# Joint heads of a hybrid S5 / RG-LRU trunk: the square behind T3's sum, a copy of Z behind the gates' sigmoids, results stored from `sq`, rows fetched back sooner, and head 9's gates on single banks

## The chip, the cores and the metric

The kernel runs on one core of one Trainium2 chip. The metric is device time in microseconds. The core has five engines that each work through their own instructions in order: TensorE (PE in the profile; its weight loads are PEld), VectorE (DVE), ScalarE (ACT), GpSimd (POOL) and SyncE (SP). They wait for one another through semaphores. SyncE and GpSimd here mostly start DMA transfers.

## The reference, cut to what matters

```python
proj = rms_norm(x, g_pre) @ w_in           # x: (1, 1024, 1024), w_in: 1024 x 5632
s5_x, s5_g, lru_x, lru_g, gate_s, gate_l = split(proj)
...
c = causal_depthwise_conv(lru_x, conv_w, conv_b)              # width 4
r = sigmoid(c_head @ w_a[head] + b_a)                         # 10 heads of 128 channels
i = sigmoid(c_head @ w_x[head] + b_x)
a = exp(-8 * r * softplus(-lam))
h = scan(h * a + sqrt(1 - a * a) * (i * c))                   # along 1024 tokens
z_l = (h * silu(lru_g)) @ w_bl
merged = sigmoid(gate_s) * z_s + sigmoid(gate_l) * z_l
x = x + rms_norm(merged @ w_out, g_post)
x = x + (p @ w_ple) * sigmoid(x @ w_ple_gate)
```

Everything is float32. The change touches only the LRU branch: the projections to `lru_x` and `lru_g`, the convolution, the gates `r` and `i`, the scan, and the way the heads' results reach the product with `w_bl`.

## The kernel before

Channels lie on the 128 partitions and the 1024 tokens in the free dimension, in two halves of 512. A 512-column float32 result fills one bank of the matmul accumulator (PSUM, 8 banks). To keep float32 accuracy every operand is split into a high part (a rounded copy made by ScalarE) and a low part (the difference, made by VectorE or by an accumulating DMA), and every product is three matmuls: high by high, high by low, low by high (`three`, L343 to 347).

**Weights.** A "quad" is four 128x128 blocks. `Weights` loads raw blocks with SyncE (L184, tile `wraw`), copies the high part on ScalarE (L246, tile `wq`), and makes the low part on VectorE (L260), or, for some, on ScalarE and GpSimd (L251, L252). `W.ahead(held)` makes quads in advance, as far as a ring of six allows; a larger `held` makes one quad fewer in advance. The instructions that it issues stand in each engine's order at that place of the program.

**Heads.** Ten heads, m = 0 to 9, run one behind the other. Heads 0, 1, 3, 4, 6 and 7 are *joint* (`joint_head`): the `lru_x` block and the `lru_g` block of a head are taken together, with the two halves of tokens, as one 2x2 block product in seven products instead of eight. Each product is a quad by 512 tokens, 12 matmuls, in this order: B11 into `c11`, T2 into `z`, B21 into `c11`, T1 into `c12`, T3 into `z`, B22 into `c12`, T4 into `z`. `c11` and `c12` are the two halves of the wide tile `hx`, `z` is the single-bank tile `hz`. Between the products sums are formed: z + u (L1358), a copy of z into `u` (ScalarE, L1359), c12 + u (L1372), and `gb` + z (VectorE, L1378), which reads T3's result before T4 adds to the same bank. `u` and `gb` are the halves of the tile `ug`. Heads 2, 5, 8 and 9 are *plain* (`plain_head`): two products of 48 matmuls each, `rx` and `rg`.

**What a head does behind its products** runs beside the products of the next head. The convolution reads `hx` (ScalarE L1268, then three steps on VectorE L1271) and gives `c`; `split` cuts it into high and low parts, `chl`. The gates are four groups of three matmuls, `pg`: the first half of tokens between T2 and B21 of the next head (in a plain head between the two halves of `rx`), the second half between T1 and T3. Their sigmoids (L1306) give `r` and `i`. Then `decay`: tanh into `ta` (L1313), exp into `r` (L1314), a square into `sq` (L1315). Then `root` (L1318, L1319), `scaled` (L1322), `scan` into `sq` (L1325) and `out`: product with the gate into `ta` (L1333), and a store of `ta` to DRAM on GpSimd's queue (L1334). `r`, `i`, `ta` and `sq` exist once, so each head waits for the one before to be done with them. `upto(n)` runs the first n of these steps, and `late` spreads them over the ticks of a plain head.

**Rows back from DRAM.** The results of heads 0 to 7 go to `yr_d`. At the start of head 9 all eight rows are fetched on GpSimd's queue (L1414) into four pages of two rows; `yr_build` splits and subtracts them (L340, L341, L1419, L1422) as operands of the product with `w_bl`, whose first four products are `bX`.

**Accumulator banks.** Pool `px` has two single banks, pool `pw2` two wide tiles (two banks each) and two single ones. The gates use `px`, except the second half of head 9, which takes a wide tile.

Of the kernel before, what the change touches and what calls it, by code (L numbers as in the profile page):

```python
# [9 lines left out]
F32 = mybir.dt.float32  # L10
F32R = mybir.dt.float32r
I32 = mybir.dt.int32
AF = mybir.ActivationFunctionType
ALU = mybir.AluOpType
# [3 lines left out]
P = 128  # L18
NT = 1024
HT = 512  # L20
ND = 8
NS = 4
NL = 10
# [14 lines left out]
JOINT = (0, 1, 3, 4, 6, 7)  # L38
# [118 lines left out]
class Weights:  # L157
# [104 lines left out]
    def next(self):  # L262
        self.make(self.pos)
        self.lows(self.pos)
        t = self.done[self.pos]
        n = QUADS[self.pos][3]
        self.pos += 1
        return [(t[:, 0, b, :], t[:, 1, b, :]) for b in range(n)]
# [10 lines left out]
def tile_hybrid_trunk(  # L279
# [10 lines left out]
    nc = tc.nc  # L290
    V, S, G, T = nc.vector, nc.scalar, nc.gpsimd, nc.tensor
# [3 lines left out]
    px = ctx.enter_context(tc.tile_pool(name="px", bufs=2, space=PSUM))  # L295
# [6 lines left out]
    def page(i, name, dt=F32R):  # L302
        return page_pool[i].tile([P, 2 * NT], dt, tag=f"pg{i}", name=name)
# [10 lines left out]
    yr_d = dram.tile([ND, P, NT], F32, name="yr_d")  # L314
# [22 lines left out]
    HALF = [slice(0, HT), slice(HT, NT)]  # L337
# [11 lines left out]
    def wide(name):  # L349
        return pw2.tile([P, NT], F32, tag="pw2", name=name)  # L350
# [6 lines left out]
    def tick():  # L357
        for g in list(bg):
            if next(g, bg) is bg:
                bg.remove(g)  # L360
# [132 lines left out]
    def xt(k, s=slice(0, NT)):  # L493
        return x_half[k // 4][:, k % 4, s]

    def two_rows(i, name, dt=F32):
        return page(i, name, dt).rearrange("p (k n) -> p k n", k=2)
# [258 lines left out]
    def square(k):  # L756
        sq = sqs[k % 2][:, k // 2 % 2] if k else ssq
        if k in (1, 3):
            (V if k == 1 else G).tensor_tensor(sq, xt(k), xt(k), ALU.mult)
        else:  # L760
            S.activation(sq, xt(k), AF.Square)
        if k:
            adds.append(sq)
# [333 lines left out]
    lop = {"T2": [3, 19], "T1": [16, 17], "T3": [2, 15], "T4": [7, 8]}  # L1097
# [45 lines left out]
    def lprod(ps, op, start, held=1):  # L1143
        W.ahead(held)
        for k, wb in enumerate(W.next()):
            three(ps, wb, (op[0][:, k, :], op[1][:, k, :]), start and k == 0, k == 3, not start)
# [20 lines left out]
    def lt(tag, name):  # L1167
        return la.tile([P, NT], F32, tag=tag, name=name)
# [35 lines left out]
    def gbank(i, name):  # L1204
        return gps.tile([P, HT], F32, tag=f"gb{i % 6}", name=name)

    for p_, m in enumerate(PAIRS):
        z = gbank(2 * p_, f"lZ{p_}") if p_ < 3 else px.tile([P, HT], F32, tag="px", name="lZ3")
# [3 lines left out]
        u = lu[:, p_]  # L1212
# [20 lines left out]
    def single(name):  # L1233
        return pw2.tile([P, HT], F32, tag="one", name=name)

    yl, yl_raw = {}, {}
    yr = []
    chl_page = page(6, "chl").rearrange("p (s n) -> p s n", s=2)
    gpage = two_rows(9, "gpage")
    ug = lt("ug", "ug")  # L1240
    u, gb = (ug[:, HALF[i]] for i in range(2))
# [14 lines left out]
    class Head:  # L1256
# [38 lines left out]
        def gates(self, h):  # L1295
            m = self.m
            if h == 0:
                self.held = W.next()
                self.r, self.i = lt("r", f"r{m}"), lt("i", f"i{m}")
            both = wide(f"pg{m}{h}") if h and m == NL - 1 else None  # L1300
            pss = [px.tile([P, HT], F32, tag="px", name=f"pg{m}{h}") if both is None else both[:, HALF[n]]
                   for n in range(2)]
            for ps, b in zip(pss, self.held):
                three(ps, b, (self.chl[:, 0, HALF[h]], self.chl[:, 1, HALF[h]]), True, True)
            for ps, t, bias in zip(pss, (self.r, self.i), (b_a, b_x)):
                S.activation(t[:, HALF[h]], ps, AF.Sigmoid, bias=bias[:, m:m + 1])  # L1306
            if h:
                V.tensor_tensor(self.i, self.i, self.c, ALU.mult)

        def decay(self):  # L1310
            m = self.m
            self.ta, self.sq = lt("ta", f"ta{m}"), lt("sq", f"sq{m}")
            S.activation(self.ta, self.r, AF.Tanh, scale=sp8[:, m:m + 1])  # L1313
            S.activation(self.r, self.r, AF.Exp, scale=nsp8[:, m:m + 1])  # L1314
            S.activation(self.sq, self.r, AF.Square)  # L1315

        def root(self):
# [9 lines left out]
        def out(self):  # L1327
            m = self.m
            if self.last:
                yl_raw[m] = lb[0].tile([P, NT], F32, tag=f"yr{m}", name=f"yr{m}")  # L1330
                V.tensor_tensor(yl_raw[m], self.sq, self.g, ALU.mult)
            else:
                V.tensor_tensor(self.ta, self.sq, self.g, ALU.mult)  # L1333
                G.dma_start(yr_d[m], self.ta)  # L1334

        def upto(self, n):
            while self.at < n:
                (self.decay, self.root, self.scaled, self.scan, self.out)[self.at]()
                self.at += 1

        def late(self):
            for n in (1, 2, 4, 5):
                self.upto(n)
                yield

    heads = {}

    def joint_head(m):
        head, prev, old = heads[m], heads.get(m - 1), heads.get(m - 2)
        xw, z = wide(f"hx{m}"), single(f"hz{m}")  # L1350
        c11, c12 = (xw[:, HALF[i]] for i in range(2))
        lprod(c11, hq["B11"], True)
        S.activation(u, c11, AF.Copy)
        if prev:
            prev.split()
        tick()
        lprod(z, lop["T2"], True)
        V.tensor_tensor(z, z, u, ALU.add)  # L1358
        S.activation(u, z, AF.Copy)  # L1359
        if old:  # L1360
            old.upto(4)
        if prev:
            prev.gate()
            prev.gates(0)
        tick()
        lprod(c11, hq["B21"], False, 1 + bool(prev))
        if old:
            old.upto(5)
        tick()
        lprod(c12, lop["T1"], True, 1 + bool(prev))  # L1370
        S.activation(gb, c12, AF.Copy)
        V.tensor_tensor(c12, c12, u, ALU.add)  # L1372
        if prev:
            prev.gates(1)
            prev.upto(1)
        tick()
        lprod(z, lop["T3"], False)
        V.tensor_tensor(gb, gb, z, ALU.add)  # L1378
        tick()
        lprod(c12, hq["B22"], False)  # L1380
        head.conv(xw, (lambda: prev.upto(2)) if prev else lambda: None)
        tick()
        lprod(z, lop["T4"], False)
        if prev:
            prev.upto(3)
        tick()
        head.parts = [(HALF[1], gb), (HALF[0], z)]

    def plain_head(m):
        head, prev, old = heads[m], heads.get(m - 1), heads.get(m - 2)  # L1390

        def between(q):
            if q:
                prev.gates(1)
                bg.append(prev.late())
                return False
            old.upto(5)
            if not prev.last:
                prev.gate()
            prev.gates(0)  # L1400
            return True

        if prev.unsplit:
            bg.insert(0, prev.first())
        head.conv(rows(hplain, f"rx{m}", between=between))
        bg.append(head.early())
        head.parts = [(slice(0, NT), rows(hplain, f"rg{m}"))]
        if head.last:
            head.gate()

    def yr_row(k):
        if k % 2 == 0:
            yr.append(two_rows(6 + k // 2, f"yr{k // 2}"))
        G.dma_start(yr[k // 2][:, k % 2], yr_d[k])  # L1414

    def yr_build():
        for k in range(4):
            bsplit("B11", k, bq(11, k))
            V.tensor_tensor(bq(11, k), bq(12, k), bq(11, k), ALU.subtract)  # L1419
            yield  # L1420
        for k in range(4):
            V.tensor_tensor(bq(12, k), bq(22, k), bq(12, k), ALU.subtract)  # L1422
            yield

    for m in range(NL):
        heads[m] = Head(m)
        if m == JOINT[-1] + 1:
            tctx.close()
            lb.append(lctx.enter_context(tc.tile_pool(name="lb", bufs=1)))
        if m == NL - 1:  # L1430
            heads[m - 2].upto(5)
            for k in range(ND):
                yr_row(k)
            bop("B11", 2, 3)
            bg.append(yr_build())
        (joint_head if m in JOINT else plain_head)(m)
# [9 lines left out]

    def between(q):
        if q == 0:
            heads[NL - 2].upto(5)
            for h in range(2):  # L1450
                heads[NL - 1].gates(h)
            bg.append(heads[NL - 1].late())
# [174 lines left out]
    for p_ in range(4):  # L1627
        m, u = 2 * p_, bu[:, p_, :]
# [8 lines left out]
        z, w_, v = (bank(f"b{n}{p_}") for n in "ZWV")  # L1637
# [202 lines left out]
    for p_ in range(4):  # L1840
        u, c21, c22 = mixt(2 * p_, 1), mixt(2 * p_ + 1, 0), mixt(2 * p_ + 1, 1)
# [173 lines left out]
```

## Time and profile before

| | us |
|---|---|
| median of 3 runs | 934.56 |
| lowest and highest run | 933.51, 934.73 |
| the profiled execution | 935.66 |
| its span, first to last instruction | 933.9 |
| TensorE busy in the span | 903.8 (97%) |
| VectorE busy | 694.0 (74%) |
| ScalarE busy | 524.9 (56%) |
| GpSimd busy | 132.4 (14%) |
| mean granted TensorE clock | 0.987 |

The heads run from about 301 to 575 us of the span. A matmul of 512 columns starts every 0.227 us when nothing is in its way. In rows of the timeline the first two numbers are the start and the time taken in us; then come the engine, the line, the operation, the tiles (out<-in), their shapes and how many instructions the row merges. In square brackets is how long the engine had been idle before, and what ended that. In the view of waits the three numbers are the total, the times and the longest, in us.

### The profile page before, as it was taken

How to read it: one execution, taken by the hardware profiler on the slowest of the kernel's cores; microseconds unless marked ns; L12 is line 12 of the kernel's file. 1: busy time of each engine (PE TensorE's matmuls, PEld its weight loads, DVE VectorE, ACT ScalarE, POOL GpSimd, SP SyncE). 2: the span in 40 equal slices, each digit the busy share in tenths (PEclk: the TensorE clock that was granted, in tenths of full speed). 3: DMA queues.
4: the chain of work that ended last, by engine and by line, in shares of the span. 5: the costliest groups of instructions: out<-in, count | busy, mean ns of one | idle time of the engine just before them, and what ended most of it. 6: DMA issues, size and time to landing. Idle time of an engine off the chain costs nothing.

```text
span 933.9 us, 11840 instructions
## 1 busy us (share of the span) xinstructions
PE 903.8 (97%) x4108; PEld 743.9 (80%) x4108; DVE 694.0 (74%) x1135; ACT 524.9 (56%) x825; POOL 132.4 (14%) x154
## 2 busy tenths in 40 slices
PE   8999999999999999889988989999999999999998
PEld 6888888888788878678767877888888888887886
DVE  6988988899745566677777777877873698786863
ACT  6644345546744486775777677544534256558531
POOL 1311000011000000000000100012322115422100
PEclk9999999999999999999989999999999999999999
DMA  9776776666654321332222255731469976499951
GB/s 358 302 254 168 230 223 182 195 177 209 167 170 147 100 70 46 97 96 74 68 67 85 97 202 158 248 135 35 158 216 268 240 200 214 120 235 242 273 200 58
DMA packets 80620, 158.34 MB, mean 170 GB/s; under 512 B 19376, under 2 KB 33840, under 8 KB 80560
## 3 DMA queue, kind: packets, MB, share of 16 engines
q1 hardware_dynamic: 54208, 112.10, 35.9%
q0 software_dynamic: 10656, 24.12, 11.7%
q10 hardware_dynamic: 15696, 21.37, 7.8%
q8 instruction: 32, 0.52, 0.2%
q14 instruction: 28, 0.23, 0.1%
HBM read 105.78 MB, written 35.91 MB: 152 GB/s over the span
## 4 chain that ended last, share of the span: by engine, by line
PE 66%; issue 15%; ACT 7%; DVE 7%; DMA 3%; POOL 1%; SPq 0%; POOLq 0%; ACTq 0%; DVEq 0%
PE ps_L L347 9%; PE ps_L L345 4%; PE ps_pg L347 3%; PE ps_F L347 3%; PE ps_u L347 3%; PE bZ L347 3%; PE lZ L347 2%; PE bW L347 2%; PE bX L347 2%; PE ps_pg L345 2%; PE hz L347 2%; PE ps_rx L347 2%; PE ps_ea L347 2%; PE ps_eb L347 2%; PE ps_F L345 2%
## 5 line engine op out<-in xcount | busy, mean ns | idle before, releaser
L246 ACT ACTIVATE wq<-wraw 128x512 fp32r<-128x512 f32 (+1 forms) x192 | 115.1, 612 | 42.2 <-DMA wraw<-w_blocks 12.0
L260 DVE TENSOR_TENSOR wq<-wraw,wq 128x512 fp32r<-128x512 f32 (+1 forms) x136 | 94.9, 706 | 36.3 <-ACT wq L246 36.2
L347 PE MATMUL ps_L<-hB,wq 128*128 128x512 f32 x384 | 119.3, 392 | 0.0
L252 POOL DMA_DIRECT2D wq<-wraw x56 | 49.3, 885 | 274.0 <-ACT wq L251 195.7
L347 PEld LDWEIGHTS ps_L<-hB,wq 128*128 128x128 f32 x384 | 72.9, 190 | 15.3
L345 PE MATMUL ps_L<-hB,wq 128*128 128x512 f32 x192 | 76.4, 398 | 0.0
L347 PE MATMUL ps_pg<-x1hl,wq 128*128 128x512 f32 x240 | 74.6, 392 | 0.9 <-DVE x1hl L1691 0.5
L347 PEld LDWEIGHTS ps_pg<-x1hl,wq 128*128 128x128 f32 x240 | 44.7, 188 | 11.7 <-DVE x1hl L1691 2.0
L347 PE MATMUL hz<-lT,wq 128*128 128x512 f32 x144 | 49.5, 428 | 0.0
L345 PE MATMUL ps_pg<-x1hl,wq 128*128 128x512 f32 x120 | 46.9, 391 | 0.0
L345 PE MATMUL hz<-lT,wq 128*128 128x512 f32 x72 | 31.4, 435 | 14.4 <-DVE ug L1378 14.4
L347 PE MATMUL hx<-hB,wq 128*128 128x512 f32 x144 | 44.5, 390 | 0.0
L345 PEld LDWEIGHTS ps_L<-hB,wq 128*128 128x128 f32 x192 | 36.4, 190 | 7.4
L347 PE MATMUL ps_u<-hB,wq 128*128 128x512 f32 x128 | 39.8, 392 | 0.4 <-DVE hB L787 0.4
L347 PE MATMUL ps_rg<-hB,wq 128*128 128x512 f32 x128 | 39.9, 393 | 0.0
L347 PE MATMUL ps_rx<-hB,wq 128*128 128x512 f32 x128 | 39.4, 389 | 0.0
L347 PE MATMUL ps_F<-ys,wq 128*128 128x512 f32 x128 | 39.4, 389 | 0.0
L260 DVE TENSOR_TENSOR wq<-wS,wq 128x512 fp32r<-128x512 f32 x50 | 35.6, 716 | 5.0 <-ACT wq L246 5.0
L246 ACT ACTIVATE wq<-wS 128x512 fp32r<-128x512 f32 x50 | 31.2, 626 | 8.8 <-POOL wS L217 7.6
L347 PEld LDWEIGHTS hz<-lT,wq 128*128 128x128 f32 x144 | 30.4, 211 | 6.7
L251 ACT ACTIVATE wq<-wraw 128x512 fp32r<-128x512 f32 x56 | 34.7, 620 | 0.0
L347 PEld LDWEIGHTS hx<-hB,wq 128*128 128x128 f32 x144 | 27.3, 190 | 5.7
(428 smaller groups left out, 2349.8 us busy)
## 6 DMA issues: line engine op xcount, KB each, us to landing
wraw<-w_blocks SPq DMA_DIRECT2D x99, 512.0 KB
wq<-wraw POOLq DMA_DIRECT2D x56, 256.0 KB, 4.1
xt<-x_t SPq DMA_DIRECT2D x8, 512.0 KB
ple_d<-ple_sb SPq DMA_DIRECT2D x8, 512.0 KB
h_d<-xt SPq DMA_DIRECT2D x8, 512.0 KB
wn<-sbt ACTq DMA_DIRECT2D x8, 512.0 KB
wn<-pt_d ACTq DMA_DIRECT2D x16, 256.0 KB
fT<-h_d ACTq DMA_DIRECT2D x4, 1024.0 KB
```

Of the source, the lines that this page charges most:

```text
L246: nc.scalar.activation(hi, src, AF.Copy)
L251: nc.scalar.activation(lo, src, AF.Copy, scale=-1.0)
L252: nc.gpsimd.dma_start(lo.bitcast(F32), src, accum_op=ALU.add)
L260: self.nc.vector.tensor_tensor(lo, src, hi.bitcast(F32), ALU.subtract)
L345: T.matmul(ps, wh, xh, start=start, stop=False, skip_group_check=more)
L347: T.matmul(ps, a, b, start=False, stop=stop and a is (wh if xl_last else wl), skip_group_check=more)
```

## The change

There are five edits.

- `square` becomes a step of its own. In a joint head T3 now leaves one more quad unmade (`held` is 2), the sum L1378 (now L1379) follows, and the square comes behind both. The steps' numbers rise by one.
- The copy of z into `u` (L1359, now L1365) moves behind the gate's and the first gates' sigmoids.
- `out` multiplies in place, in `sq`, and stores `sq` on SyncE's queue, not `ta` on GpSimd's.
- The rows are fetched page by page: rows 2 to 5 at the start of head 8, rows 0 and 1 behind head 7's second gates, rows 6 and 7 at the start of head 9. `yr_build` takes them in the order 2, 3, 0, 1.
- The second gates of head 9 use two single banks of `pw2`.

On VectorE, in head 1 as the current and head 0 as the one whose gates are formed, from c12's sum on (`hx`, `hz`: this head's products; `i`, `c`, `ta`, `sq`: head 0; `wq`: weights):

```order
-L1372 TENSOR_TENSOR hx_2991<-hx_2991,ug 128x512
-L1308 TENSOR_TENSOR i_3035<-i_3035,c_2964 128x1024
-L260 TENSOR_TENSOR wq_3100<-wraw_2917,wq_3100 128x512
-L1378 TENSOR_TENSOR ug<-ug,hz_2992 128x512
-L260 TENSOR_TENSOR wq_3102<-wraw_2974,wq_3102 128x256
-L1318 SCALAR_TENSOR_TENSOR ta_3095<-sq_3096,ta_3095 128x1024
+L1373 TENSOR_TENSOR hx_2991<-hx_2991,ug 128x512
+L1307 TENSOR_TENSOR i_3034<-i_3034,c_2964 128x1024
+L1379 TENSOR_TENSOR ug<-ug,hz_2992 128x512
+L260 TENSOR_TENSOR wq_3099<-wraw_2917,wq_3099 128x512
+L260 TENSOR_TENSOR wq_3115<-wraw_2974,wq_3115 128x256
+L1319 SCALAR_TENSOR_TENSOR ta_3095<-sq_3096,ta_3095 128x1024
```

The sum into `ug` stood behind the low part of a weight and now stands ahead of it. On ScalarE at the same place, before:

```order
L1315 ACTIVATE sq_3096<-r_3034 128x1024
L246 ACTIVATE wq_3100<-wraw_2917 128x512
L246 ACTIVATE wq_3102<-wraw_2974 128x256
L246 ACTIVATE wq_3118<-wraw_2917 128x512
L1268 ACTIVATE c_3135<-hx_2991,cp_t 128x1024
```

and now:

```order
L246 ACTIVATE wq_3099<-wraw_2917 128x512
L1316 ACTIVATE sq_3096<-r_3033 128x1024
L246 ACTIVATE wq_3115<-wraw_2974 128x256
L246 ACTIVATE wq_3117<-wraw_2917 128x512
L1268 ACTIVATE c_3135<-hx_2991,cp_t 128x1024
```

The square has changed places with the copy of the next product's weight; the five instructions are otherwise the same. On ScalarE in head 3, around the first gates (`gpage`: the gate of head 2, `pg`: its gates' products):

```order
 L1292 ACTIVATE gpage<-ps_rg_3260 128x1024
-L1306 ACTIVATE r_3375<-pg_3377,cp_t 128x512
-L1306 ACTIVATE i_3376<-pg_3378,cp_t 128x512
+L1305 ACTIVATE r_3374<-pg_3376,cp_t 128x512
+L1305 ACTIVATE i_3375<-pg_3377,cp_t 128x512
+L1365 ACTIVATE ug<-hz_3339 128x512
```

The copy out of `hz`, which stood ahead of the gate (L1359), now stands behind `r` and `i`. On SyncE, the stores of heads 0 and 1 among the loads of weights:

```order
 L184 DMA wraw_3216<-w_blocks 128x1024
+L1335 DMA yr_d<-sq_3096 128x1024
 L184 DMA wraw_3218<-w_blocks 128x1024
 L184 DMA wraw_3307<-w_blocks 128x256
-L184 DMA wraw_3446<-w_blocks 128x1024
+L1335 DMA yr_d<-sq_3280 128x1024
+L184 DMA wraw_3442<-w_blocks 128x1024
```

A store now stands between loads that followed each other directly. The diff, cut to its core:

```diff
-            both = wide(f"pg{m}{h}") if h and m == NL - 1 else None
-            pss = [px.tile([P, HT], F32, tag="px", name=f"pg{m}{h}") if both is None else both[:, HALF[n]]
-                   for n in range(2)]
+            both = h and m == NL - 1
+            pss = [single(f"pg{m}{h}") if both else px.tile([P, HT], F32, tag="px", name=f"pg{m}{h}") for _ in range(2)]
...
             S.activation(self.r, self.r, AF.Exp, scale=nsp8[:, m:m + 1])
+
+        def square(self):
             S.activation(self.sq, self.r, AF.Square)
...
-                V.tensor_tensor(self.ta, self.sq, self.g, ALU.mult)
-                G.dma_start(yr_d[m], self.ta)
+                V.tensor_tensor(self.sq, self.sq, self.g, ALU.mult)
+                nc.sync.dma_start(yr_d[m], self.sq)
...
         V.tensor_tensor(z, z, u, ALU.add)
-        S.activation(u, z, AF.Copy)
         if old:
-            old.upto(4)
+            old.upto(5)
         if prev:
             prev.gate()
             prev.gates(0)
+        S.activation(u, z, AF.Copy)
         tick()
...
-        lprod(z, lop["T3"], False)
+        lprod(z, lop["T3"], False, 1 + bool(prev))
         V.tensor_tensor(gb, gb, z, ALU.add)
+        if prev:
+            prev.upto(2)
         tick()
...
                 prev.gates(1)
                 bg.append(prev.late())
+                if prev.m == JOINT[-1]:
+                    yr_rows(0)
                 return False
...
-    def yr_row(k):
-        if k % 2 == 0:
-            yr.append(two_rows(6 + k // 2, f"yr{k // 2}"))
-        G.dma_start(yr[k // 2][:, k % 2], yr_d[k])
+    def yr_rows(n):
+        yr[n] = two_rows(6 + n, f"yr{n}")
+        for i in range(2):
+            G.dma_start(yr[n][:, i], yr_d[2 * n + i])
...
-        for k in range(4):
+        for k in (2, 3, 0, 1):
             bsplit("B11", k, bq(11, k))
...
+            yr_rows(1)
+            yr_rows(2)
         if m == NL - 1:
-            heads[m - 2].upto(5)
-            for k in range(ND):
-                yr_row(k)
+            heads[m - 2].upto(6)
+            yr_rows(3)
```

More of the change, by code (lines that the diff above doesn't have):

```diff
@@ L1236, in tile_hybrid_trunk @@
     yl, yl_raw = {}, {}
-    yr = []
+    yr = {}
     chl_page = page(6, "chl").rearrange("p (s n) -> p s n", s=2)
@@ L1332, in out @@
             else:
-                V.tensor_tensor(self.ta, self.sq, self.g, ALU.mult)
-                G.dma_start(yr_d[m], self.ta)
+                V.tensor_tensor(self.sq, self.sq, self.g, ALU.mult)
+                nc.sync.dma_start(yr_d[m], self.sq)
         def upto(self, n):
             while self.at < n:
-                (self.decay, self.root, self.scaled, self.scan, self.out)[self.at]()
+                (self.decay, self.square, self.root, self.scaled, self.scan, self.out)[self.at]()
                 self.at += 1
         def late(self):
-            for n in (1, 2, 4, 5):
+            for n in (2, 3, 5, 6):
                 self.upto(n)
@@ L1367, in joint_head @@
         if old:
-            old.upto(5)
+            old.upto(6)
         tick()
@@ L1376, in joint_head @@
         tick()
-        lprod(z, lop["T3"], False)
+        lprod(z, lop["T3"], False, 1 + bool(prev))
         V.tensor_tensor(gb, gb, z, ALU.add)
+        if prev:
+            prev.upto(2)
         tick()
         lprod(c12, hq["B22"], False)
-        head.conv(xw, (lambda: prev.upto(2)) if prev else lambda: None)
+        head.conv(xw, (lambda: prev.upto(3)) if prev else lambda: None)
         tick()
@@ L1384, in joint_head @@
         if prev:
-            prev.upto(3)
+            prev.upto(4)
         tick()
@@ L1395, in between @@
                 bg.append(prev.late())
+                if prev.m == JOINT[-1]:
+                    yr_rows(0)
                 return False
-            old.upto(5)
+            old.upto(6)
             if not prev.last:
@@ L1448, in between @@
         if q == 0:
-            heads[NL - 2].upto(5)
+            heads[NL - 2].upto(6)
             for h in range(2):
```

## The prediction

> **What bounds the kernel now.** I read the waits of TensorE first, cut to the stretch from 300 to 600 us in which the ten LRU heads run. The columns are total us, times, longest.
>
> ```profile
> PE hz L345 <- DVE ug L1378: 14.4, 5, 3.2
> PE pg L345 <- ACT r L1306: 4.5, 3, 2.8
> PE pg L345 <- DVE g L1293: 2.2, 1, 2.2
> ```
>
> Five times, once in each joint head behind the first, T4 stands before VectorE's sum L1378, which must read T3's result out of `hz` before T4 may add to it. Then I read busy time by stretches (busy us of PE, PEld, DVE, ACT, POOL, then the granted TensorE clock and DMA).
>
> ```profile
> 300.00:600.00 300.00, 278.99 (x1174) 227.09 (x1173) 214.18 (x247) 209.66 (x286) 18.14 (x27) 0.96 0.34 106
> 338.96:342.37 3.41, 1.54 (x8) 0.97 (x7) 2.49 (x4) 3.39 (x6) 0.00 (x0) 1.00 0.00 0
> 342.37:345.79 3.42, 3.42 (x10) 2.68 (x9) 3.35 (x4) 2.80 (x4) 0.00 (x0) 0.50 0.12 38
> 495.97:499.39 3.42, 1.72 (x8) 1.10 (x6) 0.10 (x1) 3.38 (x5) 0.00 (x0) 1.00 0.48 153
> 499.39:502.80 3.41, 2.07 (x9) 1.78 (x10) 3.41 (x5) 3.38 (x5) 0.00 (x0) 1.00 0.15 41
> ```
>
> TensorE is the bound: 279.0 of 300 us busy, 21.0 idle, and the clock's 0.04 below 1 costs another 12 us (give or take 1.5 for the rounding). So 33 us of this stretch are lost. The four short rows show how an idle spell lowers the clock: 1.54 us busy in a 3.41 us stretch is followed by a stretch at half clock, which loses 1.7 us; 1.72 us busy is not. I take it that 1.8 us of idleness within one such stretch is the point. **A page speaks against these rows.** The Trainium skill, "TensorE: Matmul & The Clock Gate", section "HAM oscillation — how this bites in real kernels", sets the rule that only gaps above about 3.4 us matter. The 1.87 us wait quoted next brought half clock, so the trace disagrees.
>
> **The change, T4's wait.** I worked through head 1's stage. TensorE: T3, B22, T4, and the next head's first product.
>
> ```profile
> 333.84 0.39 PE L345 MATMUL hz<-lT,wq 128*128 128x512 f32 x1
> ...
> 336.56 0.39 PE L345 MATMUL hx<-hB,wq 128*128 128x512 f32 x1
> ...
> 341.32 0.47 PE L345 MATMUL hz<-lT,wq 128*128 128x512 f32 x1 [1.87 <-DVE ug L1378]
> ...
> 345.67 0.45 PE L345 MATMUL ps_rx<-hB,wq 128*128 128x512 f32 x1
> ```
>
> ScalarE and VectorE in the same stage:
>
> ```profile
> 333.36 0.69 ACT L1306 ACTIVATE r<-pg,cp_t 128x512 f32<-128x512 f32 x1
> ...
> 337.08 1.15 ACT L1314 ACTIVATE r<-r,nsp 128x1024 f32<-128x1024 f32 x1
> 338.27 1.06 ACT L1315 ACTIVATE sq<-r 128x1024 f32<-128x1024 f32 x1
> 339.24 1.44 ACT L246 ACTIVATE wq<-wraw 128x512 fp32r<-128x512 f32 x3
> 340.58 1.19 ACT L1268 ACTIVATE c<-hx,cp_t 128x1024 f32<-128x1024 f32 x1
> ```
>
> ```profile
> 334.77 1.23 DVE L1308 TENSOR_TENSOR i<-i,c 128x1024 f32<-128x1024 f32 x1 [0.75 <-ACT i L1306]
> 339.88 0.69 DVE L260 TENSOR_TENSOR wq<-wraw,wq 128x512 fp32r<-128x512 f32 x1 [3.89 <-ACT wq L246]
> 340.49 0.68 DVE L1378 TENSOR_TENSOR ug<-ug,hz 128x512 f32<-128x512 f32 x1
> 341.09 0.42 DVE L260 TENSOR_TENSOR wq<-wraw,wq 128x256 fp32r<-128x256 f32 x1
> 341.42 1.22 DVE L1318 SCALAR_TENSOR_TENSOR ta<-sq,ta 128x1024 f32<-128x1024 f32 x1
> 342.56 3.91 DVE L1271 SCALAR_TENSOR_TENSOR c<-hx,cp_t,c 128x1023 f32<-128x1023 f32 x3
> ...
> 348.72 0.69 DVE L217 TENSOR_TENSOR wS<-wraw 128x512 f32<-128x512 f32 x1
> 349.44 0.69 DVE L217 TENSOR_TENSOR wS<-wS,wraw 128x512 f32<-128x512 f32 x1
> 350.06 1.28 DVE L341 TENSOR_TENSOR chl<-c,chl 128x512 fp32r<-128x512 f32 x2
> ```
>
> A product of 12 matmuls takes 336.56 - 333.84 = 2.72 us. Today the sum is queued on VectorE behind a weight's low part, which idles 3.89 us for ScalarE: exp ends at 338.2, the square follows, and only then the weight's copy. With one weight fewer made ahead of T3, the sum comes first: L1308 ends at 336.0, T3 at 336.6, so the sum runs from about 336.8 to 337.5. B22 ends at 336.56 + 2.72 = 339.28, so T4 no longer waits. It also loses its slow clock: today T4 takes 345.67 - 341.32 = 4.35 us. The weight that is made later is still in time: copied behind exp, its low part is done by 339.5, and T4 covers it until 342.0.
>
> **What is late next: the gates.** T4 would run 339.28 to 342.00, the next head's first 24 matmuls to 347.44, and then the gates' first half. Its second matmul, at 347.67, is the first to read the low part of `chl`, the convolution's split output. ScalarE does the same work ahead of `c` in another order, so `c` still starts at 340.5 and ends at 341.7. VectorE is rid of the sum there: low part at 338.8, the 0.42 one behind its copy at about 340.1, `ta` 340.4 to 341.6, convolution at 341.7 instead of 342.56, 0.87 earlier. What stands between convolution and `chl` is unchanged, so `chl`'s first half ends at 350.06 + 0.69 - 0.87 = 349.9 (0.69 as the other 128x512 rows), and with the 0.15 us from 341.17 (the sum's end) to 341.32 TensorE goes on at 350.0. **A new wait of 2.35 us** stands where none was. Said generally: from `r` (333.36) to that second matmul TensorE has 14.31 us of work, and the chain needs 16.7.
>
> Head 4 has the same list of instructions (2.4, a trifle for `r`, which must wait for the scan of the head before). Head 7 lacks the two additions L217, 1.4 us, which leaves 1.0. Heads 3 and 6:
>
> ```profile
> 385.90 0.70 ACT L1306 ACTIVATE r<-pg,cp_t 128x512 f32<-128x512 f32 x1
> ...
> 402.16 1.29 DVE L341 TENSOR_TENSOR chl<-c,chl 128x512 fp32r<-128x512 f32 x2 [0.31 <-ACT chl L340]
> ```
>
> 402.16 + 0.69 - 385.90 = 16.95, less 0.87, plus 0.15, is 16.2; against 14.31 about 1.8 is left, 1.7 because part of the 0.31 goes too. Five new waits: 2.35 + 1.7 + 2.4 + 1.7 + 1.0 = **9.15 us**. The ends for this unknown: nothing, if the chain shortens by more than I see, and T4's present 14.4 us if it shortens by nothing.
>
> Half clock: the waits of 2.35 and 2.4 hold 1.8 us of idleness within one 3.41 us stretch in about 6 of 10 positions (TensorE's idle time is some 0.15 less than the wait: (1.6 + 0.4) / 3.41). I take one such stretch, 1.7 us; the ends are none and five. The other three waits are too short. By the rule of the Trainium skill named above none of the five would lower the clock, which would give 1.7 us less.
>
> **Copy of Z behind the sigmoids.** In heads 3 and 6 ScalarE is held by that copy:
>
> ```profile
> 379.89 0.60 ACT L1359 ACTIVATE ug<-hz 128x512 f32<-128x512 f32 x1 [5.62 <-DVE hz L1358]
> ```
>
> The sigmoids that free the gates' banks stood behind it; they now run within these 5.62 us. So the two shorter waits on `r` go: 4.5 - 2.8 = 1.7 us. T3, which overwrites what the copy reads, comes three products later (2.72 + 2.72 + 1.36 = 6.8 us behind the gates), which hides the move; without that cover T3 would wait for the copy's 0.60 us.
>
> **Rows fetched sooner.** Head 8's gates waited 2.8 us because ScalarE stood at a split of fetched rows:
>
> ```profile
> 540.70 0.63 ACT L340 ACTIVATE bB<-yr 128x512 fp32r<-128x512 f32 x1 [9.36 <-DMA yr<-yr_d]
> ```
>
> The rows that this split reads first are now asked for when head 7's T4 frees their pages, so a plain head ahead: 24 + 24 + 48 matmuls and two gates are 21.8 + 2.7 = 24.5 us. The 2.8 us go. **Head 9 on single banks:** its second gates no longer wait for the wide tile that L1293 releases; the pool's single banks were last used by head 7. The 2.2 us go, and what follows (L7's second half, 24 matmuls or 5.4 us) covers the reading of the singles before bX0 writes there.
>
> **Sum.** All 33 us go; 9.15 of new waits and 1.7 of half clock come: 33 - 10.85 = 22.15. Against the profiled execution: 935.66 - 22.15 = 913.5. The median of the runs lies 1.1 below that execution, so **912.4 us**.
>
> **Rivals.**
> *The new wait doesn't come* (chance 0.10): if VectorE or ScalarE have slack that I did not see, 33 us go: 934.56 - 33 = 901.6. Against it: every row of head 1's chain follows its predecessor without a gap.
> *The wait only moves* (0.14): every new wait is 1 us longer and lowers the clock: 9.15 + 5 + 5 x 1.7 = 22.65, gain 10.3, 924.2. For it: ScalarE and VectorE get fuller when the stretch shrinks; the 1.7 us waits are only 0.3 from the point. That the early fetch does nothing, because a page comes free later than I think, would cost 2.8 + 1.7 alone, within the range.
> *No half clock follows* (0.04): if waits this short leave the clock alone, 9.15 us come and no more: 33 - 9.15 = 23.85, 910.7. The stretch with 1.54 us busy, which brought half clock, speaks against it. That is what the rule in the Trainium skill, "TensorE: Matmul & The Clock Gate", would make of these waits.
> *Slower: the stores on SyncE's queue* (0.04). Each store of a head's rows now stands between weight loads, and the next square, in the same `sq`, waits for it on ScalarE. Head 1's loads on either side, and the product it stores:
>
> ```profile
> 372.80 6.25 SPq L184 DMA_DIRECT2D wraw<-w_blocks  x2
> ...
> 376.82 1.22 DVE L1333 TENSOR_TENSOR ta<-sq,gpage 128x1024 f32<-128x1024 f32 x1
> ```
>
> ```profile
> yr_d<-ta POOLq DMA_DIRECT2D x7, 512.0 KB, 2.9
> ```
>
> The load ahead went at 372.80, before the product ended at 378.04; the one behind at 372.80 + 6.25 - 0.33 = 378.72. The store fits between. The square comes at least T1, gates and T3 later (6.8 us), the store needs 2.9. It would decide from a store held 3.9 us, and the kernel would be slower once all eight were held 3.9 + 22.15 / 8 = 6.7 us; at 10 us each the time is 912.4 + 8 x 6.1 = 961.
>
> **Chances.** 0.68 for the forecast, whose own range is 908 to 917. The range for 8 in 10 takes in most of the moved wait and part of the missing one: 905 to 922. What this kernel's measurement can tell from no change is 0.2%, 1.9 us: faster 0.94, same 0.02, slower 0.04.
>
> **What would show it.** The profile after should have no wait of `hz` on the sum; a wait of `pg` on `chl` (L341), five times, 1 to 2.5 us, about 9 in all, first at the gates of head 1; one or two stretches at clock 0.50 where there were seven (12 / 1.7); no wait of `pg` on `r` or `g`; on ScalarE no square waiting for a store. The forecast is wrong if T4 still waits, if `chl` waits 3 us or more each time, or if loads on SyncE land late and `wq` appears among TensorE's waits.

## The result, and the profile after

| | before | after |
|---|---|---|
| median, us | 934.03 (4 runs, 933.44 to 934.73) | 913.03 (4 runs, 912.93 to 913.75) |
| ratio after to before | | 0.9776, 95% interval 0.976 to 0.9793 |
| the profiled execution, us | 935.66 | 913.0 |
| span, us | 933.9 | 911.2 |

The kernel is 21.0 us faster, where 22.15 was forecast; the time, 913.03, stands 0.6 us from the predicted 912.4. Between the two profiled executions, from which the forecast was worked out, the gain is 22.7 us. The agreement hides errors in what each edit was held to be worth, which the experiments bring out.

TensorE's waits after the change, from 300 to 600 us (total, times, longest):

```profile
PE pg L347 <- DVE chl L341: 7.8, 5, 2.1
```

This one line stands where three stood. T4 waits no more for the sum, and the gates no more for `r` or `g`; the gates wait five times for the low part of `chl`. The engines' busy times by stretches (PE, PEld, DVE, ACT, POOL, clock, DMA):

```profile
300.00:600.00 300.00, 292.23 (x1277) 240.19 (x1276) 230.91 (x266) 217.38 (x297) 18.35 (x23) 0.99 0.39 120
347.35:350.76 3.41, 1.34 (x7) 0.79 (x5) 3.38 (x6) 2.40 (x3) 0.00 (x0) 1.00 0.53 154
350.76:354.18 3.42, 3.42 (x10) 2.64 (x9) 3.38 (x3) 0.92 (x2) 0.00 (x0) 0.50 0.00 0
419.02:422.43 3.41, 3.04 (x14) 2.19 (x12) 3.41 (x5) 2.75 (x5) 0.00 (x0) 1.00 0.27 56
422.43:425.84 3.41, 1.70 (x7) 1.42 (x8) 3.38 (x5) 1.07 (x2) 0.00 (x0) 1.00 0.26 102
```

TensorE idles 7.8 of the 300 us, down from 21.0, and the mean clock there is 0.99 after 0.96. The next two rows are head 1's gates, with the only stretch at half clock that is left; the last two are head 4's. Head 1's stage on TensorE (T4's first product, then the gates), and on VectorE:

```profile
339.80 0.39 PE L345 MATMUL hz<-lT,wq 128*128 128x512 f32 x1
...
347.96 0.39 PE L345 MATMUL pg<-chl,wq 128*128 128x512 f32 x1
350.42 0.95 PE L347 MATMUL pg<-chl,wq 128*128 128x512 f32 x2 [2.07 <-DVE chl L341]
```

```profile
337.28 0.69 DVE L1379 TENSOR_TENSOR ug<-ug,hz 128x512 f32<-128x512 f32 x1 [0.77 <-PE hz L347]
...
342.18 3.92 DVE L1271 SCALAR_TENSOR_TENSOR c<-hx,cp_t,c 128x1023 f32<-128x1023 f32 x3
346.01 0.68 DVE L260 TENSOR_TENSOR wq<-wraw,wq 128x512 fp32r<-128x512 f32 x1
346.61 1.22 DVE L1323 TENSOR_TENSOR i<-i,ta 128x1024 f32<-128x1024 f32 x1
347.74 0.69 DVE L260 TENSOR_TENSOR wq<-wraw,wq 128x512 fp32r<-128x512 f32 x1
348.34 0.69 DVE L217 TENSOR_TENSOR wS<-wraw 128x512 f32<-128x512 f32 x1
349.07 0.69 DVE L217 TENSOR_TENSOR wS<-wS,wraw 128x512 f32<-128x512 f32 x1
349.68 1.29 DVE L341 TENSOR_TENSOR chl<-c,chl 128x512 fp32r<-128x512 f32 x2
```

The sum now ends at 337.97, ahead of T4 at 339.80. The gates' second matmul, due 0.23 us after 347.96, starts at 350.42, 2.23 us late, against 2.35 foretold. Between the convolution, which ends at 346.10, and `chl` stand five instructions of other work: the chain's rows follow each other without a gap.

### The profile page after: what moved, and what is told of

The parts are those of the page before. It is cut to its first block, busy times and chain, and to the rows that moved or that the text cites. A ratio compares the mean times of both kernels' runs of the same rounds, so it can differ in the third digit from the quotient of the medians.

```text
span 911.2 us, 11843 instructions
## 1 busy us (share of the span) xinstructions
PE 895.1 (98%) x4108; PEld 739.0 (81%) x4108; DVE 694.1 (76%) x1135; ACT 524.4 (58%) x825; POOL 126.9 (14%) x146
## 4 chain that ended last, share of the span: by engine, by line
PE 80%; DVE 8%; ACT 5%; issue 3%; DMA 2%; POOL 0%; SPq 0%; ACTq 0%; POOLq 0%; DVEq 0%
PE ps_L L347 9%; PE ps_pg L347 6%; PE ps_L L345 5%; PE ps_rg L347 3%; PE ps_F L347 3%; PE ps_u L347 3%; PE bZ L347 3%; PE ps_pg L345 3%; PE hx L347 3%; PE lZ L347 2%; PE ps_rx L347 2%; PE bX L347 2%; PE bW L347 2%; DVE c L1271 2%; PE pg L347 2%
## 5 line engine op out<-in xcount | busy, mean ns | idle before, releaser
L347 PE MATMUL hz<-lT,wq 128*128 128x512 f32 x144 | 44.3, 389 | 0.0
L1305 ACT ACTIVATE r<-pg,cp_t 128x512 f32<-128x512 f32 x20 | 13.8, 692 | 35.4 <-PE pg L347 19.1
L347 PE MATMUL pg<-chl,wq 128*128 128x512 f32 x80 | 25.9, 406 | 7.8 <-DVE chl L341 7.8
```

The source lines that it names most:

```text
L347: T.matmul(ps, a, b, start=False, stop=stop and a is (wh if xl_last else wl), skip_group_check=more)
```

## The experiments

The diffs are against the changed kernel, but for the copy moved alone, which is against the kernel before, and for two experiments that build on the one above them (`sq` stored from GpSimd's queue, and the scan behind the scaling), which are against that one. Times are medians, and ratios are against the kernel before on the same chip. The experiments ran on several chips, on which the kernel before took 934.0 to 934.7 us, so a difference between two of the times is uncertain by about 0.7 us, beside the intervals.

**T3's edit undone.** The square right behind exp, and `held` back to 1 at T3.

```diff
-        lprod(z, lop["T3"], False, 1 + bool(prev))
+        lprod(z, lop["T3"], False)
         V.tensor_tensor(gb, gb, z, ALU.add)
-        if prev:
-            prev.upto(2)
...
             prev.gates(1)
-            prev.upto(1)
+            prev.upto(2)
```

> The changed kernel with its T3 part taken back (square right behind exp, one weight more made ahead of T3); all else of the change stays. Theory (T4 and chl are two waits on one chain, and the later one counts): T4 waits about 2.0 us again in each of the five heads, conv starts 0.87 us later, and the waits for chl shrink from 7.8 to about 3 us; 915.5 to 919 us, so the T3 part alone is worth 3 to 6 us. Rival (the T4 waits of before, 14.4 us with their half clock, were the gain): they come back in full and the time is 924 us or more.

918.14 us (917.12 to 918.38), ratio 0.9823 (0.9808 to 0.9837). TensorE's waits:

```profile
PE hz L345 <- DVE ug L1379: 9.4, 5, 1.9
PE pg L347 <- DVE chl L341: 1.6, 2, 0.8
```

T4's wait is back, with 1.9 us in each of five heads, 9.4 in all, and not the 14.4 of before. So 5 us of T4's waits had another cause. What T3's edit is worth beside the others is 918.14 - 913.03 = 5.1 us (4.4 by the ratios). It was not run alone in the kernel before, so what it would have removed there by itself is not shown.

**Its two halves.** First the square alone put back behind exp (`held` stays 2), then `held` alone put back (the square stays behind the sum).

```diff
-        if prev:
-            prev.upto(2)
...
-            prev.upto(1)
+            prev.upto(2)
```

> The changed kernel with only the square put back right behind exp; T3 still leaves one weight more unmade. Theory (what held the sum was the weight's low part ahead of it in VectorE's queue, not the square): no wait of hz, conv about 0.3 us later, chl waits about 9 us in all; 913 to 916 us. Rival (the square on ScalarE was what T4 waited for): T4 waits 1 us or more in five heads and the time is 918 us or more.

914.88 us (914.1 to 916.45), ratio 0.9792 (0.9777 to 0.9807):

```profile
PE pg L347 <- DVE chl L341: 9.1, 5, 2.4
```

```diff
-        lprod(z, lop["T3"], False, 1 + bool(prev))
+        lprod(z, lop["T3"], False)
```

> The changed kernel with only the number of weights made ahead of T3 put back; the square stays behind the sum. Theory (a short wait at T4 is repaid by the shorter wait for chl behind it): T4 waits about 0.9 us in each of five heads, the waits for chl fall from 7.8 to about 3.3 us, the time stays at 911 to 914 us. Rival (waits add up): 913 + 4.6 = 917 us or more.

910.63 us (910.43 to 911.32), ratio 0.9746 (0.9731 to 0.976):

```profile
PE hz L345 <- DVE ug L1379: 2.4, 3, 0.8
PE pg L347 <- DVE chl L341: 2.0, 2, 1.0
PE hz L345 <- ACT sq L1316: 1.6, 2, 0.8
```

With the quad held back alone, T4's wait is gone, and the low part of `chl` is waited for 1.3 us longer in all. With the square moved alone, T4 waits 0.8 us five times, and that delay is time in which `chl` gets nearer: `chl` is waited for 2.0 us (3.3 were expected), and all waits come to 6.0 us against 7.8, none long enough to lower the clock. The second quad held back frees T4 of these last 0.8 us, as the prediction had it, but with it the kernel is 2.4 us slower: five short waits at T4 cost less here than longer ones at the gates, one of which lowers the clock. Most of it is the clock. Matmul by matmul, the kernel with the square alone moved is 0.05 us ahead of the changed kernel where the latter's half-clock stretch begins, 1.6 us ahead where it ends, and 2.1 us behind head 7's gates.

**The copy of Z back ahead of the gates.**

```diff
         V.tensor_tensor(z, z, u, ALU.add)
+        S.activation(u, z, AF.Copy)
         if old:
             old.upto(5)
         if prev:
             prev.gate()
             prev.gates(0)
-        S.activation(u, z, AF.Copy)
```

> The changed kernel with the copy of Z put back ahead of the gates. Theory (the copy delays r in heads 3 and 6 by 2.5 us, and with r the whole chain to chl, so it costs more than the gates' 1.7 us): pg waits on r 0.8 us twice, the waits for chl of heads 3 and 6 grow from 1.57 to about 3 us, with half clock behind them; 919 to 923 us. Rival (the copy costs only the waits of pg on r, as my sum had it): 913 + 1.7 + 0.3 = 915 us.

921.38 us (920.25 to 922.56), ratio 0.9864 (0.9847 to 0.988): 8.35 us, where the prediction's step would give 1.7. ScalarE in head 3 with the copy back:

```profile
380.55 0.60 ACT L1360 ACTIVATE ug<-hz 128x512 f32<-128x512 f32 x1 [5.63 <-DVE hz L1359]
381.15 1.28 ACT L1292 ACT_TABLE_LOAD   x1
382.45 1.03 ACT L1292 ACTIVATE gpage<-ps_rg 128x1024 f32<-128x1024 f32 x1
...
386.55 0.70 ACT L1305 ACTIVATE r<-pg,cp_t 128x512 f32<-128x512 f32 x1
```

and in the changed kernel, from the same table load to the same second `r`:

```profile
375.01 1.28 ACT L1292 ACT_TABLE_LOAD   x1
...
380.62 0.60 ACT L1365 ACTIVATE ug<-hz 128x512 f32<-128x512 f32 x1 [1.72 <-DVE hz L1359]
...
383.40 0.60 ACT L1372 ACTIVATE ug<-hx 128x512 f32<-128x512 f32 x1 [0.62 <-PE hx L347]
384.09 0.69 ACT L1305 ACTIVATE r<-pg,cp_t 128x512 f32<-128x512 f32 x1
```

The copy runs at the same time in both. But the table load and the sigmoids that stood behind it now run in the idle time ahead of it, so the second half's `r`, from which tanh, exp, the convolution and `chl` follow in ScalarE's order, comes at 384.09, not 386.55. ScalarE even has 0.62 us to spare there. TensorE's waits in the kernel with the copy back:

```profile
PE pg L347 <- DVE chl L341: 9.2, 5, 2.1
PE pg L345 <- ACT r L1305: 1.6, 2, 0.8
PE pg L345 <- ACT chl L340: 0.8, 2, 0.4
```

Its 11.6 us of waits are 3.8 more than the 7.8. Its trace has two stretches at half clock (from 351.18 and from 402.38), the changed kernel's has one, which adds 1.7 us: 5.5 of the 7.3 us between the two spans (918.5 and 911.2). The other 1.8 us stay open. The median lies 1.1 us above this profiled execution (920.25), whose granted clock, 0.996, is the highest of the four (the others have 0.994 to 0.991); so more half clock in the others is likely, but they have no trace.

**The copy moved in the kernel before, and nothing else.**

```diff
         V.tensor_tensor(z, z, u, ALU.add)
-        S.activation(u, z, AF.Copy)
         if old:
...
             prev.gates(0)
+        S.activation(u, z, AF.Copy)
```

> The kernel before with the copy of Z moved behind the gates' sigmoids and nothing else. Theory (the copy delays r of heads 3 and 6's gates and the chain behind it, T4's square included): the gates' waits in those heads go, 1.1 us each, T4's waits there shrink from about 3.3 to 2.0, and some half clock goes with them: 926 to 930. Rival (only the gates' two waits go): about 932.

927.74 us (925.9 to 928.03), ratio 0.992 (0.9906 to 0.9933), 7.0 us. T4's first row in heads 1, 3, 4, 6 and 7, before and then with the copy moved:

```profile
341.32 0.47 PE L345 MATMUL hz<-lT,wq 128*128 128x512 f32 x1 [1.87 <-DVE ug L1378]
393.76 0.77 PE L345 MATMUL hz<-lT,wq 128*128 128x512 f32 x1 [3.19 <-DVE ug L1378]
420.39 0.47 PE L345 MATMUL hz<-lT,wq 128*128 128x512 f32 x1 [3.10 <-DVE ug L1378]
472.81 0.77 PE L345 MATMUL hz<-lT,wq 128*128 128x512 f32 x1 [3.18 <-DVE ug L1378]
500.73 0.47 PE L345 MATMUL hz<-lT,wq 128*128 128x512 f32 x1 [3.04 <-DVE ug L1378]
```

```profile
341.84 0.47 PE L345 MATMUL hz<-lT,wq 128*128 128x512 f32 x1 [1.87 <-DVE ug L1378]
391.34 0.47 PE L345 MATMUL hz<-lT,wq 128*128 128x512 f32 x1 [1.87 <-DVE ug L1378]
417.00 0.77 PE L345 MATMUL hz<-lT,wq 128*128 128x512 f32 x1 [3.22 <-DVE ug L1378]
466.95 0.47 PE L345 MATMUL hz<-lT,wq 128*128 128x512 f32 x1 [1.87 <-DVE ug L1378]
493.04 0.47 PE L345 MATMUL hz<-lT,wq 128*128 128x512 f32 x1 [2.46 <-DVE ug L1378]
```

In heads 3 and 6 the wait falls from 3.2 to 1.87 us: the copy made the rest. Head 4 keeps its longer wait and head 7 half of what it had beyond 1.87, and the next experiment says what that is.

**The results from `ta` and on GpSimd's queue again.**

```diff
-                V.tensor_tensor(self.sq, self.sq, self.g, ALU.mult)
-                nc.sync.dma_start(yr_d[m], self.sq)
+                V.tensor_tensor(self.ta, self.sq, self.g, ALU.mult)
+                G.dma_start(yr_d[m], self.ta)
```

> The changed kernel with the product written to ta and stored on the queue of GpSimd again. Theory: in heads 4 and 7 tanh of the next head, which writes ta, waits about 1.4 us for the store to land, and the chain to chl is late by as much; 913.0 + 2.8, with or without a half clock more: 914.5 to 918 us. Rival (the two waits of tanh lie in slack): 913 us.

916.78 us (915.2 to 917.04), ratio 0.9809 (0.9795 to 0.9823), 3.75 us for an edit costed at nothing. TensorE's waits, then ScalarE's row in head 4:

```profile
PE pg L347 <- DVE chl L341: 9.6, 5, 3.0
```

```profile
410.05 1.15 ACT L1312 ACTIVATE ta<-r,sp 128x1024 f32<-128x1024 f32 x1 [1.22 <-DMA yr_d<-ta]
```

The next head's tanh writes into `ta`, and waits 1.22 us until the store has read it; `chl` comes that much later. In head 7 it is 1.17 us. The waits for `chl` grow by 1.8 us in all, and this trace has a second stretch at half clock, behind head 4's wait of 3.0 us. The kernel before has the same row, in heads 4 and 7 alone:

```profile
413.70 1.15 ACT L1313 ACTIVATE ta<-r,sp 128x1024 f32<-128x1024 f32 x1 [1.12 <-DMA yr_d<-ta]
...
494.04 1.15 ACT L1313 ACTIVATE ta<-r,sp 128x1024 f32<-128x1024 f32 x1 [1.06 <-DMA yr_d<-ta]
```

This is the rest of T4's longer waits there: they exceed 1.87 us by 1.23 and 1.17. With only the copy moved, the excess in head 4 is 1.35 us and that in head 7 is 0.59, and tanh waits for the store 1.22 us in head 4 and in head 7 only this:

```profile
486.34 1.16 ACT L1313 ACTIVATE ta<-r,sp 128x1024 f32<-128x1024 f32 x1 [0.48 <-DMA yr_d<-ta]
```

So the two go together, though the stores were not moved alone in the kernel before. The product in `sq` takes it away, since `sq` is written later in the next head than `ta`. That it is the tile and not the queue shows below: with `sq` stored from GpSimd's queue, `chl` is waited for 7.7 us, as in the changed kernel.

**All eight rows fetched at head 9's start, as before.**

```diff
-            yr_rows(1)
-            yr_rows(2)
         if m == NL - 1:
             heads[m - 2].upto(6)
-            yr_rows(3)
+            for n in range(4):
+                yr_rows(n)
...
-                if prev.m == JOINT[-1]:
-                    yr_rows(0)
...
-        for k in (2, 3, 0, 1):
+        for k in range(4):
```

> The changed kernel with all eight rows fetched at the start of head 9 again, in the old order. Theory: ScalarE stands at the split of the first row, head 8's second gates wait 2.8 us for r, half clock follows; 913.0 + 2.8 + 1.7 = 917.5 us (916 to 918.5). Rival (the fetch is hidden anyway now that stores go out sooner on SyncE): 913 us.

913.34 us (913.16 to 914.2), ratio 0.9777 (0.9764 to 0.9791): the theory falls. TensorE's only wait is `chl`'s 7.8 us, and GpSimd's rows say why:

```profile
503.49 3.17 POOL L1417 DMA_DIRECT2D yr<-yr_d  x6 [22.85 <-PE pg L347]
520.27 0.53 POOL L1417 DMA_DIRECT2D yr<-yr_d  x1 [13.61 <-DVE sq L1334]
```

Six of the eight are out by 506.66, 13.6 us ahead of the seventh, from the same place in the program: no store stands ahead of them among GpSimd's instructions any more. In the kernel before, all eight went out from 534.93 on, directly behind the last store.

**The same, with `sq` stored from GpSimd's queue.**

```diff
-                nc.sync.dma_start(yr_d[m], self.sq)
+                G.dma_start(yr_d[m], self.sq)
```

> The changed kernel with the eight rows fetched in one go at head 9's start, as before, and the stores of sq issued from GpSimd instead of SyncE. Theory (in the kernel before the fetch was late since it stood on GpSimd's queue behind head 7's store, not since it was asked for late): the store comes back onto that queue, the fetch behind it, and head 8's gates wait for r some 2.8 us with a stretch of half clock behind: 913.3 + 4.5 = about 917.5 (916 to 919). Rival (the queue that stores are issued from does not matter for the fetch): no wait on r and 913.3, within 0.7.

917.14 us (916.92 to 917.6), ratio 0.9806 (0.9793 to 0.982). GpSimd, and TensorE's waits:

```profile
520.60 0.55 POOL L1335 DMA_DIRECT2D yr_d<-sq  x1 [20.49 <-PE pg L347]
521.15 4.17 POOL L1417 DMA_DIRECT2D yr<-yr_d  x8
```

```profile
PE pg L347 <- DVE chl L341: 7.7, 5, 2.1
PE pg L345 <- ACT r L1305: 2.6, 1, 2.6
```

All eight fetches stand behind the last store, and the wait on `r` is back, with a stretch at half clock behind it (from 530.09). With the fetch early, or with the stores on SyncE's queue, it is gone; only with neither does it stand. Each edit alone is enough.

**Head 9's second gates on the wide tile again.**

```diff
-            both = h and m == NL - 1
-            pss = [single(f"pg{m}{h}") if both else px.tile([P, HT], F32, tag="px", name=f"pg{m}{h}") for _ in range(2)]
+            both = wide(f"pg{m}{h}") if h and m == NL - 1 else None
+            pss = [px.tile([P, HT], F32, tag="px", name=f"pg{m}{h}") if both is None else both[:, HALF[n]]
+                   for n in range(2)]
```

> The changed kernel with head 9's second gates in a wide tile again. Theory: they wait for VectorE's product with the gate that releases the wide tile. That product follows head 8's r by 21 us, and TensorE now comes there sooner since nothing slows it in between, so the wait is 2.9 us, not the 2.2 of before; with half clock 913.0 + 4.6 = 917.6 us (916 to 918.5). Rival (the wait is what it was): 2.2 us, 917 us or less. Second rival (later slack hides it): 913 us.

915.78 us (913.33 to 917.18), ratio 0.9799 (0.978 to 0.9817), 2.75 us. Beside the waits on `chl`, unchanged, TensorE has this one:

```profile
PE pg L345 <- DVE g L1293: 1.9, 1, 1.9
```

The wait is 1.9 us and no half clock follows it in this profile, where the theory had 2.9 us and half clock: it is about what it was before (2.2), the rival's answer. Only these 1.9 us are shown to be the edit's. The four runs spread from 913.33 us (granted clock 0.999) to 917.18 (0.995), and the trace is of the slowest: it has a second stretch at half clock, from 424.65, at head 4's gates, which the edit does not touch.

**Past both kernels: the split ahead of other work.** The five instructions between convolution and `chl` are there by program order alone. `split` goes right behind T4, ahead of the old head's scaling (L1323) and the weights of the tick.

```diff
         lprod(z, lop["T4"], False)
+        head.split()
         if prev:
             prev.upto(4)
         tick()
```

> The changed kernel with the split of the convolution's output moved ahead of the product i*ta and of the next weights on VectorE, right behind T4's weights. Theory (the wait for chl is now the bound, and VectorE's order sets it): chl comes 1.8 us sooner in heads 3 and 6 and 3.2 us sooner in the others, the waits of pg on chl all but go, 1 to 2 us of other waits appear in heads 4 and 7 where ScalarE's r is late; 902 to 906 us. Rival (the wait only moves, since ScalarE now stands at the copy of chl until the convolution ends): 909 us or more.

**904.83 us** (904.69 to 905.08), ratio 0.9685 (0.9672 to 0.9698). VectorE in head 1, and TensorE's waits:

```profile
346.83 1.29 DVE L341 TENSOR_TENSOR chl<-c,chl 128x512 fp32r<-128x512 f32 x2 [0.16 <-ACT chl L340]
```

```profile
PE pg L345 <- ACT chl L340: 0.9, 2, 0.4
PE pg L347 <- DVE chl L341: 0.5, 2, 0.2
```

`chl` starts 2.85 us sooner (349.68 - 346.83), and 8.2 us of the time go: 6.4 us of waits, and the half clock, of which none is left. In heads 4 and 7 a little is left, since `r` there waits for the scan of the head before. So as a last step `prev.upto(4)` becomes `prev.upto(5)` in the same place, which puts that scan right behind the scaling:

```diff
         head.split()
         if prev:
-            prev.upto(4)
+            prev.upto(5)
```

> The version with head.split() ahead of the old head's scan (904.83), and in addition the old head's scan moved right behind the scaling in T4's stage, so that r of heads 4 and 7's gates no longer has it ahead. Theory: the remaining 2.4 us of excess in heads 4 and 7 go: about 902.5 (902 to 904.5). Rival: what remains hangs on ScalarE's own order, and the scan ahead makes the combine of the old head later: 904.8 or more.

**903.66 us** (903.52 to 904.27), ratio 0.9663 (0.965 to 0.9676), the best of all:

```profile
PE hx L347 <- DVE wq L260: 1.2, 2, 0.6
```

The waits of heads 4 and 7 are gone; heads 3 and 6 wait 0.6 us each for a weight's low part, which now comes behind the scan on VectorE.

## Why the prediction was right, and where only its sum was

- **The bound, right.** What TensorE loses between 300 and 600 us is what the kernel can gain. Its waits fell by 13.3 us, and of the seven half-clock stretches, about 1.7 us each, one is left: 13.3 + 10.2 = 23.5 us, against 22.7 between the two spans. The sum, 935.66 - 22.15 = 913.5, is 0.5 us above the profiled execution (913.0). The 1.1 us taken off for the median did not hold after the change: median and profiled execution are the same there.
- **The new waits, right.** Foretold were 2.35, 1.7, 2.4, 1.7 and 1.0 us for heads 1, 3, 4, 6 and 7. Start to start, less 0.23, they are 2.23, 1.56, 2.24, 1.56 and 0.96: each within 0.16, all a little shorter. (For heads 3 and 6 the step's own figures leave 16.2 - 14.31 = 1.9 us, not 1.8, ahead of its last correction.) Following one chain by its rows from `r` to `chl`, against TensorE's work in matmuls, gave five numbers that no trace had shown.
- **One half-clock stretch, right in size, and by luck in number.** Of the two long waits one brought it. Which does hangs on where they fall: with the same five waits, the trace of the late fetch has its one stretch at head 4 (from 423.90), and that of the wide tile has two.
- **T4's wait, mis-sized as a term of T3's edit.** The step gave that edit all of 14.4 us and their half clock. Its own part of the waits is 5 x 1.87 = 9.4. The longer waits of heads 3 and 6 (1.3 us each) were the copy's, those of heads 4 and 7 (1.2 each) the store's, in head 7 together with the copy. The step was worked out in head 1, where neither is, and carried over to the rest; that the longest wait was 3.2 and head 1's 1.87 stood in the prediction's own rows.
- **The copy of Z, mis-sized: 1.7 us against 8.35 (undone) or 7.0 (alone).** The step counted only the wait next to the copy. What it missed is behind it on ScalarE: 2.46 us on the way to `r`, and so to everything that follows from it.
- **The stores, mis-sized: nothing against 3.75.** The step looked at the queue that they join and at the tile that they now hold, and not at `ta`, which they set free.
- **Rows fetched sooner: the amount right, the cause one of two.** With neither edit the wait is 2.6 us with one half-clock stretch, where 2.8 and 1.7 us were counted. The wait went, but the stores' move to SyncE alone would have taken it.
- **Head 9, right in the wait:** 2.2 us against 1.9. Whether half clock follows it, as in the profile before, the runs of the wide tile do not settle.

Undone one by one, the edits are worth 5.1 + 8.35 + 3.75 + 0.3 + 2.75 = 20.25 us of the 21.0 by the times, but 17.9 by the ratios, which set off one chip against another. That this comes near 21.0 shows little, since such amounts need not add up: the fetch counts for nothing here only because the stores cover for it. The total was right all the same, as I read it, because each wait was removed by some edit of the five, and what replaced them was worked out from the chain that remains, whichever edit had shortened it. For the copy alone the step would have missed by 5 us.

The rival "the new wait doesn't come" needs the split in another place: 903.66 is near its 901.6. The rival with longer waits, 924.2, did not come: none of the five was longer than forecast. Stores on SyncE as a loss did not show: no square waits for one.

## What to carry to other kernels

A wait that stands five times need not have one cause: where its lengths differ from place to place, follow each length back, since the excess belongs to other edits. An instruction that idles on an in-order engine costs not its own consumer alone but the start of every chain queued behind it, and a tile written late in the next stage is a better place for a result to be stored from than one that is written early. When a wait has moved to the end of a chain, look for the instructions that stand in it by program order alone: here two moved lines gave 9.4 us more.

## What the runs showed of the hardware

The half clock goes by stretches of fixed length that run on regardless of the work. In the kernel before, it begins at 342.37, 393.57, 420.88, 472.08 (two stretches in a row), 543.76 and 567.65 us; counted from the first, the others lie 15, 23, 38, 59 and 66 times 3.413 us later. After the change, head 1's half-clock stretch starts at 350.76; 21 x 3.413 = 71.67 us later, at 422.43, one of these stretches begins within head 4's wait. Two waits of 2.07 and 2.08 us then differ in effect: head 1's lies in one stretch, of which 1.34 us are busy, and half clock follows; head 4's is cut by the boundary, with 3.04 and 1.70 us busy, and none follows. In the kernel before, 1.54 us busy brought half clock; with the quad held back alone, 1.56 us (348.70 to 352.11) did not. So the point lies at about 1.55 us busy of 3.41, or 45%, and at 1.86 us of idleness, where the prediction took 1.8.

This holds for a stretch at full clock. In the kernel before, the stretch from 472.08 to 475.49 ran at half clock, was busy for 2.68 us, and was followed by another at half clock; those busy for 3.2 us or more at half clock were not. It would fit if busy time at half clock counted half (1.34 us), but that rests on this one case.

The Trainium skill, "TensorE: Matmul & The Clock Gate", section "What's actually happening", has such a free-running window of 3413 ns, and the trace agrees; the rule of the Trainium skill that the prediction names, that only gaps above 3.4 us matter, it contradicts a second time, with 2.07 us.
